# First modulation in four quarters of 256 features, each followed by its share of the latent projections

## The chip, the core and the metric

One core of a Trainium2 chip runs the kernel. The metric is the device time of one execution in microseconds; a time without a qualifier is the median of several runs. Engines are named as in the profile: PE is TensorE (matmuls; PEld its weight loads), DVE is VectorE, ACT is ScalarE, POOL is GpSimd, SP is SyncE, which here issues nearly all transfers from memory.

## The reference, cut to what matters

One layer over 256 latent and 256 context rows of 1024 features. A conditioning vector gives a shift and a scale for each feature; these modulate the normalised rows; one wide projection of the modulated rows follows, of which the 384 query columns (latent rows only) and the 320 key/value columns (all rows) are the first to be computed here. Retention, attention, a merge and 32 experts, each token using four of them, come after.

```python
m = silu(c) @ ada_w + ada_b              # 6144 columns; the first 2048 are shift and scale of this stage
h = rms_norm(x, norm1_g) * (1 + scale) + shift        # the same for ctx with its own vector
z = h @ w_in                                          # columns 6144:6528 queries, 6528:6848 key/value
```

## The kernel before

Everything is float32. A product of the big projections is made of three fast-format products: the operand is split into a high half (rounded, on ScalarE) and a low half (the rest, on VectorE), and `mm3` issues high x high, high x low and low x high. Weights come in tiles of 128 partitions x 1024 numbers into a ring of `WR = 7` buffers. `step` collects a list of steps, some with a weight; `run_steps` walks it, starts the loads up to seven weights ahead, splits a weight shortly before its use (`split_to`; `ahead[0]` says how many beyond the next, 0 in the opening and `AHEAD = 2` later, and `ahead[1](n)` calls for splits by hand), and calls the step. The instructions of each engine run in the order in which this list issues them; SP's transfers too.

The opening is written out by hand in that list. Features are counted in eight blocks of 128 (`KD = 8`).

- `ada_half(h, ks)` computes the modulation of half of the features: for each block k one weight tile of 512 shift and 512 scale columns, and two products against `sT`, which holds the two conditioning vectors in 32 columns, into `ap0[32 * g:32 * g + 32]`, g = 2h and 2h + 1. The shift goes into one strip of 32 partitions and the scale into the next. The bias comes first as a product of `ident` and `adab` in each strip. These products aren't split: an ordinary float32 product shows as two records of the trace.
- `ada_out` copies the result out of `ap0`, `ada_mod` transposes it and forms scale and shift by feature (`mod1`), and `modulate(u, ks)` makes the high and low halves `hh`, `hl` of the modulated rows (u = 0 latent, 1 context). In the code the first of these sequences is `start1`, the second `start2`.
- `norm_rows` and `xn_transposes` normalise the rows and bring them into columns.
- `project_cq` and `project_ckv` are the query and key/value projections, in steps of two blocks k.
- `keep_clock(n)` puts n small bf16 products with unused results on TensorE (`CLK`).

The order before: half 0 of the modulation, with the rows' norm and transposes between its products; `start1`; queries k 0 to 3 and key/value k 0 to 1; half 1 of the modulation, eight tiles with four dummies after each; key/value k 2 to 3 with `start2` inside; queries k 4 to 7; the queries' norm; key/value k 4 to 7; the transposes of the normed queries (`cq_rows`); the gate columns (`C_GM`) in four steps.

Later in the kernel the spaces `first` (two tiles, heads of the attention output) and `accp` (the gates) are in use; in the opening they are free. The expert weights are loaded on SP by lines 1107 and 1112 into rings of 2 MB tiles that open as the spaces of the mixer stage close.

Of the kernel before, what the change touches and what calls it, by code (L numbers as in the profile page):

```python
# [10 lines left out]
F32 = mybir.dt.float32  # L11
# [48 lines left out]
def hybrid_block(ctx: ExitStack, tc: tile.TileContext, A, out, dbg=None):  # L60
# [152 lines left out]
    def run_steps():  # L213
# [9 lines left out]
        def split_next():  # L223
            w, nk, n, raw = loaded[len(ready)]
# [13 lines left out]
        for spec, fn in steps:  # L238
            while len(loaded) < min(at[0] + WR, len(loads) - 1):
# [14 lines left out]
    def load(src, r0, nk, pieces, raw=False):  # L254

        n = sum(p[1] for p in pieces)
        w = wtile4()
        v = w[:, :nk * n].rearrange("p (k n) -> p k n", k=nk)
        o = 0
        if len(pieces) > 1 and len({p[1] for p in pieces}) == 1 and nk == 1:  # L260
            (c0, cn), (c1, _) = pieces
            a = src[r0:r0 + 128]
            a = bass.AP(tensor=a.tensor, offset=a[:, c0:c0 + cn].offset, ap=[list(a.ap[0]), [c1 - c0, 2], [1, cn]])
            nc.sync.dma_start(w[:, :n].rearrange("p (c n) -> p c n", c=2), a)
# [5 lines left out]
        return w, nk, n, raw  # L270
# [24 lines left out]
    def ada_bias(ps, r):  # L295
        nc.tensor.matmul(ps, ident[0:12, r:r + 1].to_broadcast([12, 32]), adab, start=True, stop=False)

    def ada_half(h, ks):
        for k in ks:
            def f(w, k=k):  # L300
                if h == 0 and k == 0:
                    bank("ap0")
                ap0 = B["ap0"]
# [8 lines left out]
    def ada_out(h):  # L312
        s = slice(64 * h, 64 * h + 64)
# [4 lines left out]
    def ada_mod(h):  # L318
        s = slice(64 * h, 64 * h + 64)
        ps = pt_((128, 4, 2, 32))  # L320
        for c in range(4):
            nc.tensor.transpose(ps[:, c].rearrange("p a b -> p (a b)"), ada0[s, 128 * c:128 * c + 128], ident[s, s])
        ks = slice(4 * h, 4 * h + 4)
# [1390 lines left out]
```

## Time and profile before

| what | value |
|---|---|
| median of 3 runs (lowest, highest) | 1489.52 us (1488.69, 1493.41) |
| the profiled execution: time, span | 1487.58 us, 1485.8 us |
| mean granted clock of TensorE | 0.988 |
| busy: PE, PEld, DVE, ACT, POOL | 93%, 52%, 44%, 23%, 6% |
| memory read | 490.03 MB, 331 GB/s over the span |
| L308, products of the first modulation | 64 records, 20.2 us busy |

The busy share of PE counts matmuls that are pipelined into one another, so it doesn't tell how close the engine is to its peak. A row of a timeline gives a start and a duration in us; because matmuls overlap at their ends, the price of one is read from the distance between starts. The granted clock of the first few microseconds isn't on record: 1.00 is shown there, and the distances tell more.

### The profile page before, as it was taken

What the parts mean: (1) busy time and instruction counts of PE and PEld (TensorE: products, weight loads), DVE (VectorE), ACT (ScalarE), POOL (GpSimd) and SP (SyncE); (2) the same over time, 40 slices, a digit from 0 to 9 for tenths busy, and PEclk for the clock granted to TensorE, in tenths of its full rate; (3) what the DMA queues carried; (4) which work ended last, traced back from release to release, by engine and by line L of the source; (5) the groups of instructions that cost most, each with busy time, mean ns of one, the idle gap of its engine ahead of it and who ended that gap; (6) DMA issues with size and microseconds to landing.
All of it is one profiled execution on the core that took longest, in us unless ns stands there. A gap on an engine that the chain in (4) does not pass through costs nothing.

```text
span 1485.8 us, 18943 instructions
## 1 busy us (share of the span) xinstructions
PE 1388.0 (93%) x7859; PEld 775.8 (52%) x7859; DVE 651.5 (44%) x1111; ACT 344.4 (23%) x604; POOL 87.9 (6%) x95
## 2 busy tenths in 40 slices
PE   8998999999999989999999999989899889989986
PEld 4677888888888874333333333333333333333323
DVE  4488876757676572323322323222322232223224
ACT  4364543534443331110100101100110011001001
POOL 2201050101101030000000000000000000000000
PEclk9999999999999899999999999999999999999998
DMA  8634473554548778999999999999999999999994
GB/s 286 204 108 141 142 265 101 164 177 130 176 161 322 266 286 337 427 426 427 428 425 428 427 426 427 427 428 426 427 428 426 428 427 427 427 428 427 427 422 172
DMA packets 75077, 492.38 MB, mean 331 GB/s; under 512 B 6579, under 2 KB 16892, under 8 KB 50152
## 3 DMA queue, kind: packets, MB, share of 16 engines
q1 hardware_dynamic: 74008, 489.22, 81.8%
q0 software_dynamic: 576, 1.23, 0.3%
q8 instruction: 63, 1.03, 0.3%
q10 hardware_dynamic: 400, 0.66, 0.1%
q14 instruction: 30, 0.25, 0.0%
HBM read 490.03 MB, written 1.05 MB: 331 GB/s over the span
## 4 chain that ended last, share of the span: by engine, by line
PE 51%; DMA 40%; DVE 6%; issue 1%; ACT 1%; POOL 0%; SPq 0%; DVEq 0%; ACTq 0%
DMA w<-in_exp_w_gu_dram 26%; DMA w<-in_exp_w_down_dram 13%; PE ps L1479 11%; PE ps L286 9%; PE ps L287 9%; PE ps L285 9%; PE ps L1510 5%; PE ps L145 2%; PE ps L1340 1%; PE ps L308 1%; PE ps L1459 1%; PE ps L457 1%; DVE up L1487 1%; DVE up L1485 1%; DVE ws L277 0%
## 5 line engine op out<-in xcount | busy, mean ns | idle before, releaser
L1479 PE MATMUL ps<-w,xg 128*64 128x512 f32 x2048 | 459.8, 596 | 36.2 <-DMA w<-in_exp_w_gu_dram 33.9
L1479 PEld LDWEIGHTS ps<-w,xg 128*64 128x64 f32 x2048 | 140.5, 137 | 333.8 <-issue 253.7
L1510 PE MATMUL ps<-w,ga 128*64 128x512 f32 x992 | 218.1, 592 | 0.0
L277 DVE TENSOR_TENSOR ws<-w,ws 128x1024 fp32r<-128x1024 f32 (+2 forms) x114 | 139.2, 1230 | 66.4 <-ACT ws L276 65.3
L1466 DVE SCALAR_TENSOR_TENSOR x<-ps,gate,x 128x512 f32<-128x512 f32 x124 | 84.5, 744 | 187.2 <-PE ps L1459 187.2
L1510 PEld LDWEIGHTS ps<-w,ga 128*64 128x64 f32 x992 | 71.2, 137 | 141.9 <-issue 141.9
L1519 DVE TENSOR_TENSOR ps<-ps,gate 128x512 f32<-128x512 f32 (+1 forms) x33 | 22.6, 683 | 270.1 <-PE ps L1510 261.2
L276 ACT ACTIVATE ws<-w 128x1024 fp32r<-128x1024 f32 (+2 forms) x114 | 116.9, 1028 | 101.0 <-PE ps L287 79.5
L1484 ACT ACTIVATE ps<-ga 128x512 f32<-128x512 f32 x32 | 19.3, 602 | 471.5 <-DVE ga L1483 471.5
L286 PE MATMUL ps<-ws,hh 128*128 128x512 f32 (+3 forms) x304 | 109.5, 360 | 3.5 <-DVE ws L277 3.5
L285 PE MATMUL ps<-ws,hh 128*128 128x512 f32 (+3 forms) x304 | 110.1, 362 | 2.4 <-DVE ptl L282 2.4
L287 PE MATMUL ps<-ws,hl 128*128 128x512 f32 (+3 forms) x304 | 109.1, 359 | 0.4 <-DVE hl L383 0.4
L1483 DVE TENSOR_SCALAR ga<-ps 128x512 f32<-128x512 f32 x32 | 22.1, 692 | 161.4 <-PE ps L1479 161.4
L281 ACT ACTIVATE up<-ps 128x512 fp32r<-128x512 f32 (+1 forms) x33 | 19.3, 584 | 260.2 <-DVE ps L1519 260.1
L286 PEld LDWEIGHTS ps<-ws,hh 128*128 128x128 f32 x304 | 57.3, 188 | 13.2 <-DVE ws L277 4.9
L1340 PE MATMUL ps<-bgu,ident 128*64 128x512 f32 x256 | 63.2, 615 | 0.0
L285 PEld LDWEIGHTS ps<-ws,hh 128*128 128x128 f32 x304 | 57.1, 188 | 11.4 <-DVE ptl L282 2.7
L287 PEld LDWEIGHTS ps<-ws,hl 128*128 128x128 f32 x304 | 57.1, 188 | 9.1 <-DVE hl L383 0.7
L145 PE MATMUL ps<-ident,up 128*128 128x128 f32 x128 | 24.1, 312 | 24.0 <-DVE up L1487 24.0
L340 DVE SCALAR_TENSOR_TENSOR ada<-w,sc,ada 128x1024 f32<-128x1024 f32 x32 | 40.6, 1278 | 0.0
L1426 PE MATMUL ps<-oh,acc_m 128*128 128x128 bf16 x512 | 40.6, 224 | 0.0
L285 PE MATMUL ps<-ath,hth 128*128 128x256 f32 x128 | 35.7, 279 | 1.2 <-ACT ath L281 1.2
(383 smaller groups left out, 1820.5 us busy)
## 6 DMA issues: line engine op xcount, KB each, us to landing
w<-in_exp_w_gu_dram SPq DMA_DIRECT2D x124, 2048.0 KB, 39.1
w<-in_exp_w_down_dram SPq DMA_DIRECT2D x62, 2048.0 KB, 39.1
w<-in_ada_w_dram SPq DMA_DIRECT2D x48, 512.0 KB, 4.5
w<-in_w_in_dram SPq DMA_DIRECT2D x48, 512.0 KB, 4.5
w<-in_w_in_dram SPq DMA_DIRECT2D x32, 256.0 KB, 4.3
w<-in_w_branch_ret_dram SPq DMA_DIRECT2D x16, 512.0 KB, 5.9
w<-in_exp_w_gu_dram SPq DMA_DIRECT2D x8, 1024.0 KB, 27.1
w<-in_w_branch_mla_dram SPq DMA_DIRECT2D x8, 512.0 KB, 5.2
```

The lines of the kernel that those rows point to most:

```text
L145: nc.tensor.transpose(dst, src, ident[:n, :n])
L276: nc.scalar.activation(hi[:, :n], src, AF.Copy)
L277: nc.vector.tensor_tensor(lo[:, :n], src, hi[:, :n].bitcast(F32), op=OP.subtract)
L285: nc.tensor.matmul(ps, a[0], b[0], start=start, stop=False, skip_group_check=True)
L286: nc.tensor.matmul(ps, a[0], b[1], start=False, stop=False, skip_group_check=True)
L287: nc.tensor.matmul(ps, a[1], b[0], start=False, stop=stop, skip_group_check=True)
L340: nc.vector.scalar_tensor_tensor(a, w, sc[:, k:k + 1], a, op0=OP.mult, op1=OP.add)
L1340: nc.tensor.matmul(ps[64 * h:64 * h + 64], pick_row(c // 512).to_broadcast([128, CAP]), bgu, start=True, stop=False, skip_group_check=True)
L1426: nc.tensor.matmul(ps[:, i, :w], pairs(part[:, t], 4)[:, k // 2, k % 2], rhs, start=(t + p + i == 0), stop=(t + p == 3), skip_group_check= ...
L1466: nc.vector.scalar_tensor_tensor(a, pss[h], g[:, t:t + 1], a, op0=OP.mult, op1=OP.add)
L1479: nc.tensor.matmul(ps[64 * h:64 * h + 64], xg[k // 4][:, k % 4, sl], w[:, c:c + 512], start=False, stop=(k == KD - 1), skip_group_check=True)
L1510: nc.tensor.matmul(py[64 * h:64 * h + 64], hT[f], w[:, 1024 * r + 512 * h:1024 * r + 512 * h + 512], start=(f == 0), stop=(f == KD - 1))
```

## The change

The modulation is computed in four quarters of 256 features (`ada_quarter`) instead of two halves. A weight tile now holds two blocks k of 256 shift and 256 scale columns. Shift and scale of quarter q lie side by side in one strip, `ap0[32 * q:32 * q + 32]`, and the two products of a tile, for its two blocks k, go there one after the other. The eight bias products of 256 columns all come at the start (`ada_begin`). The first six weight tiles are placed in `first` and `accp` and don't count against the seven of the ring, so the loads run further ahead; each such tile is loaded by two transfers of 256 KB. The rows are loaded ahead of all weights.

After each quarter the two blocks k that it completes are modulated (`begin(q)`), projected for the queries, and later, between the products of the next quarter, for the key/values. The dummies of the second half and of `start1` are gone. `xn_transposes` works by pairs of blocks; `cq_rows` moves behind the first gate step. The arithmetic is the same.

```diff
-            while len(loaded) < min(at[0] + WR, len(loads) - 1):
+            while len(loaded) < len(loads) - 1 and sum(not w[4] for w in loaded[at[0]:]) < WR:
...
-        w = wtile4()
+        w = where() if where else wtile4()
...
-    def ada_half(h, ks):
-        for k in ks:
-            def f(w, k=k):
...
-                for c in range(2):
-                    g = 2 * h + c
-                    if k == 0:
-                        ada_bias(ap0[32 * g:32 * g + 32], 2 * c + h)
-                    nc.tensor.matmul(ap0[32 * g:32 * g + 32], sT[:, k], w[:, 512 * c:512 * c + 512],
-                                     start=False, stop=(k == KD - 1))
-            step(f, (A["ada_w"][0], 128 * k, 1, [(512 * h, 512), (1024 + 512 * h, 512)], True))
...
+    def ada_begin():
+        bank("ap0")
+        for q in range(4):
+            for c in range(2):
+                r = 2 * c + q // 2
+                nc.tensor.matmul(B["ap0"][32 * q:32 * q + 32, 256 * c:256 * c + 256],
+                                 ident[0:12, r:r + 1].to_broadcast([12, 32]), adab[:, 256 * (q % 2):256 * (q % 2) + 256],
+                                 start=(c == 0), stop=False, skip_group_check=True)
...
+    def early_tile(n):
+
+        if n % 2 == 0:
+            early[n // 2] = (*first, accp)[n // 2].tile([128, 2, 1024], F32, name=("w", "w", "acc_m")[n // 2])
+        return early[n // 2][:, n % 2]
+
+    def ada_quarter(q, k2s):
+
+        for k2 in k2s:
+            def f(w, k2=k2):
+                for k in range(2):
+                    nc.tensor.matmul(B["ap0"][32 * q:32 * q + 32], sT[:, 2 * k2 + k], w[:, 512 * k:512 * k + 512],
+                                     start=False, stop=(2 * k2 + k == KD - 1), skip_group_check=True)
+            step(f, (A["ada_w"][0], 256 * k2, 2, [(256 * q, 256), (1024 + 256 * q, 256)], True,
+                     (lambda n=4 * q + k2: early_tile(n)) if 4 * q + k2 < 6 else None))
...
+    def begin(q):
+
+        ks = range(2 * q, 2 * q + 2)
+        ada_mod(q)
+        if q:
+            ahead[1](0)
+        modulate(0, ks)
+        ahead[1](0 if q == 0 else 1)
+        modulate(1, ks)
...
+    step(ada_begin)
     keep_clock(CLK[0])
+    step(lambda: got.__setitem__("r1", norm_factors()))
     step(gain_cols)
+    step(stash("cq"), cq_weights(0))
+    step(lambda: norm_rows(got["r1"]))
+    for k2 in range(3):
+        ada_quarter(0, range(k2, k2 + 1))
+        keep_clock(CLK[1])
+    step(lambda: xn_transposes(0))
+    ada_quarter(0, range(3, 4))
+    step(lambda: ada_out(0))
+    step(lambda: xn_transposes(1))
+    step(lambda: begin(0))
+    step(lambda: bank(*PCQ))
+    for q in range(4):
+        if q:
+            step(stash("cq"), cq_weights(q))
+        step(lambda q=q: block(cq_jobs, q, range(2), *got["cq"]))
+        if q == 3:
+            break
+        ada_quarter(q + 1, range(0, 2))
+        if q == 0:
+            step(lambda: (xn_transposes(2), xn_transposes(3), bank(*PKV)))
+        step(stash("kv"), kv_weights(q))
+        step(lambda q=q: block(kv_jobs, q, range(1), *got["kv"]))
+        ada_quarter(q + 1, range(2, 4))
+        step(lambda q=q: ada_out(q + 1))
+        step(lambda q=q: block(kv_jobs[:2], q, range(1, 2), *got["kv"]))
+        step(lambda q=q: begin(q + 1))
+        step(lambda q=q: block(kv_jobs[2:], q, range(1, 2), *got["kv"]))
     step(lambda: ahead.__setitem__(0, AHEAD))
...
     step(cq_norm)
-    project_ckv(range(2, 4))
+    step(lambda hi, lo: block(kv_jobs, 3, range(2), hi, lo), kv_weights(3))
+    project_lat(C_GM, ("gm0", "gm1"), range(0, 1))
     step(cq_rows)
-    project_lat(C_GM, ("gm0", "gm1"), range(0, 1))
     step(ckv_norm)
```

## Rows read from the trace of the kernel before

**Rows 1.** Page, part 2: GB/s moved in 40 equal slices
```profile
GB/s 286 204 108 141 142 265 101 164 177 130 176 161 322 266 286 337 427 426 427 428 425 428 427 426 427 427 428 426 427 428 426 428 427 427 427 428 427 427 422 172
```

**Rows 2.** Page, part 4: chain that ended last, shares of the span
```profile
PE 51%; DMA 40%; DVE 6%; issue 1%; ACT 1%; POOL 0%; SPq 0%; DVEq 0%; ACTq 0%
```

**Rows 3.** Stretches: length, busy us (instructions) per engine, PEclk, DMA share, GB/s
```profile
600.00:1000.00 400.00, 384.74 (x2158) 150.06 (x2156) 120.44 (x199) 44.08 (x97) 0.00 (x0) 1.00 1.01 427
```

**Rows 4.** Stretches of the opening, the same view
```profile
4.00:30.00 26.00, 25.66 (x178) 12.41 (x178) 8.15 (x28) 11.24 (x18) 1.86 (x4) 1.00 1.01 348
...
40.40:53.80 13.40, 13.40 (x71) 3.37 (x69) 0.95 (x2) 0.74 (x1) 0.00 (x0) 1.00 0.53 169
```

**Rows 5.** TensorE's waits, 0 to 70 us: us in total, times, longest
```profile
PE ps L286 <- DVE ws L277: 2.0, 3, 0.9
...
PE ps L308 <- DMA w<-in_ada_w_dram: 0.2, 1, 0.2
```

**Rows 6.** Timeline, SP: start, us, instruction, count
```profile
461.02 5.86 SPq L1107 DMA_DIRECT2D w<-in_exp_w_gu_dram  x3
```

**Rows 7.** SP's waits, 440 to 600 us
```profile
SPq L1107 <- PE ps L287: 14.8, 4, 4.5
```

**Rows 8.** Timeline, TensorE, second half; of xN records two make a product
```profile
40.48 1.04 PE L296 MATMUL ps<-adab,ident 12*32 12x512 f32 x2
41.45 1.04 PE L308 MATMUL ps<-w,sT 128*32 128x512 f32 x2
...
44.38 0.40 PE L457 MATMUL ps<-ones 128*128 128x128 bf16 x4
44.70 1.05 PE L308 MATMUL ps<-w,sT 128*32 128x512 f32 x4
45.69 0.40 PE L457 MATMUL ps<-ones 128*128 128x128 bf16 x4
```

**Rows 9.** Timeline, TensorE, first half: two pairs, then transposes
```profile
21.20 1.91 PE L308 MATMUL ps<-w,sT 128*32 128x512 f32 x8
23.05 1.97 PE L145 MATMUL ps<-ident,x 128*128 128x128 f32 x16
```

**Rows 10.** Timeline, TensorE: two full-width products and the next line
```profile
487.98 1.88 PE L1190 MATMUL ps<-ada,one 128*128 128x512 f32 x4
489.78 1.08 PE L1195 MATMUL ps<-ada,one 128*64 128x512 f32 x4
```

**Rows 11.** Timeline, TensorE, start: product, bias product, sixty dummies
```profile
5.98 1.89 PE L308 MATMUL ps<-w,sT 128*32 128x512 f32 x2 [0.18 <-DMA w<-in_ada_w_dram]
7.80 1.91 PE L296 MATMUL ps<-adab,ident 12*32 12x512 f32 x2
...
11.49 4.06 PE L457 MATMUL ps<-ones 128*128 128x128 bf16 x60
```

**Rows 12.** Timeline, first joint: copy-out, transposes, low half, dense product
```profile
27.44 0.41 DVE L315 COPY ada<-ps 64x256 f32<-64x256 f32 x1
...
27.99 0.71 PE L322 MATMUL ps<-ident,ada 64*128 64x64 f32 x4
...
29.08 0.96 DVE L277 TENSOR_TENSOR ws<-w,ws 128x768 fp32r<-128x768 f32 x1
...
30.96 0.44 PE L287 MATMUL ps<-ws,hl 128*128 128x384 f32 x1 [0.42 <-DVE hl L383]
```

**Rows 13.** Timeline, TensorE: last two latent products
```profile
69.99 0.31 PE L286 MATMUL ps<-ws,hh 128*128 128x320 f32 x1
...
70.13 0.31 PE L287 MATMUL ps<-ws,hl 128*128 128x320 f32 x1
```

**Rows 14.** Timeline, TensorE: the fourth gate block
```profile
82.19 0.50 PE L286 MATMUL ps<-ws,hh 128*128 128x512 f32 x1 [1.50 <-DVE ws L277]
```

**Rows 15.** Timeline, TensorE: first product after an idle stretch
```profile
142.93 0.58 PE L286 MATMUL ps<-ptl,mvh 128*128 128x256 f32 x1 [2.93 <-DVE ptl L282]
```

**Rows 16.** Stretches again, here for the granted clock (PEclk)
```profile
142.00:146.00 4.00, 3.07 (x15) 3.08 (x16) 3.94 (x6) 0.32 (x1) 0.00 (x0) 0.57 0.79 265
```

More of the change, by code (lines that the diff above doesn't have):

```diff
@@ L223, in split_next @@
         def split_next():
[L224 removed]
+            w, nk, n, raw, _ = loaded[len(ready)]
             if raw:
@@ L252, in run_steps, with load @@
         steps.clear()
-    def load(src, r0, nk, pieces, raw=False):
+    def load(src, r0, nk, pieces, raw=False, where=None):
         n = sum(p[1] for p in pieces)
-        w = wtile4()
+        w = where() if where else wtile4()
         v = w[:, :nk * n].rearrange("p (k n) -> p k n", k=nk)
         o = 0
-        if len(pieces) > 1 and len({p[1] for p in pieces}) == 1 and nk == 1:
+        if len(pieces) > 1:
             (c0, cn), (c1, _) = pieces
-            a = src[r0:r0 + 128]
-            a = bass.AP(tensor=a.tensor, offset=a[:, c0:c0 + cn].offset, ap=[list(a.ap[0]), [c1 - c0, 2], [1, cn]])
-            nc.sync.dma_start(w[:, :n].rearrange("p (c n) -> p c n", c=2), a)
+            for k in range(nk):
+                a = src[r0 + 128 * k:r0 + 128 * k + 128]
+                a = bass.AP(tensor=a.tensor, offset=a[:, c0:c0 + cn].offset, ap=[list(a.ap[0]), [c1 - c0, 2], [1, cn]])
+                nc.sync.dma_start(v[:, k].rearrange("p (c n) -> p c n", c=2), a)
         else:
@@ L269, in load @@
                 o += cn
-        return w, nk, n, raw
+        return w, nk, n, raw, where
     def split(src, n):
@@ L357, in norm_rows, with xn_transposes @@
                 nc.vector.tensor_scalar(xt, xt, r1[:, t:t + 1], None, op0=OP.mult)
-    def xn_transposes(u):
-        for k2 in range(KD // 2):
+    def xn_transposes(k2):
+        for u in range(2):
             ps = pt_((128, 2, 256))
@@ L385, in modulate, with project, block @@
                 nc.gpsimd.dma_start(dbg["hT"][:, k, s], hf)
-    def project(pieces, jobs, kks, mid=None, at=None):
+    def project(pieces, jobs, kks):
         for k2 in kks:
-            def f(hi, lo, k2=k2):
-                for k in range(2):
-                    kk = 2 * k2 + k
-                    for n, (name, cut, t, a, b, first) in enumerate(jobs):
-                        if mid and at == (k, n):
-                            mid()
-                        s = slice(128 * t, 128 * t + 128)
-                        mm3(cut(B[name]), (hh[:, kk, s], hl[:, kk, s]), (hi[:, k, a:b], lo[:, k, a:b]),
-                            start=(kk == 0 and first), stop=(kk == KD - 1))
-            step(f, (A["w_in"][0], 256 * k2, 2, pieces))
+            step(lambda hi, lo, k2=k2: block(jobs, k2, range(2), hi, lo), (A["w_in"][0], 256 * k2, 2, pieces))
+    def block(jobs, k2, ks, hi, lo):
+        for k in ks:
+            kk = 2 * k2 + k
+            for name, cut, t, a, b, first in jobs:
+                s = slice(128 * t, 128 * t + 128)
+                mm3(cut(B[name]), (hh[:, kk, s], hl[:, kk, s]), (hi[:, k, a:b], lo[:, k, a:b]),
+                    start=(kk == 0 and first), stop=(kk == KD - 1))
     def whole(p):
```

83 lines of the change are left out of this document (24 added, 59 removed).

## The prediction

> **What bounds the kernel now.** I read the slices of the span first, then the opening stretch by stretch, then who made TensorE wait there, then single instructions. In the slices [rows 1] the transfers run near 427 GB/s only from about the sixteenth slice on; before that they move 100 to 340 GB/s. The chain of work that ended last says the same: about half TensorE, four tenths transfers of expert weights [rows 2]. So there are two regimes, an opening and a mixer bound by the order written for TensorE, and then an expert stage bound by bytes (427 GB/s, transfers busy all the time [rows 3]).
>
> The change lies wholly in the first 75 us. There TensorE is busy for 25.66 of the 26 us from 4 to 30 and for all of the 13.4 us from 40.4 to 53.8, while the transfers make 348 and 169 GB/s [rows 4]. Before 70 us it waited 0.2 us for a weight of the first modulation, and 2.0 us for split weights [rows 5]. The opening is thus bound by how long TensorE's list is, not by the weights' arrival: whatever the change gains by earlier transfers has next to nothing to remove. What counts is whether the new list is longer.
>
> Does a longer opening reach the end? The expert transfers are issued on SP when space falls free: the first three at 461 us, in 5.9 us [rows 6], and between 440 and 600 us SP waited 14.8 us for TensorE's last mixer products before issuing four of them [rows 7]. So the start of the byte-bound regime moves with TensorE, and I carry a delay of the opening to the end one to one.
>
> **The change, part by part.** All prices are of the profiled execution: span 1485.8, time 1487.58 us.
>
> (a) The modulation's products. A product here has 32 columns of stationary data and 512 columns to stream. Before, line 308 issues two for each weight tile, into different strips of 32 partitions. At full clock such a pair takes 0.98 us when something else stands ahead of it (44.70 to 45.69), and two pairs in a row take 1.85 (21.20 to 23.05), so each further one 0.86 [rows 8, 9]. A lone one takes 0.97 (40.48 to 41.45, a bias product of 512 columns; the two of line 308 beside it take as long) [rows 8]. So the second of a pair is free: the strips run side by side. After the change the two products of a tile go into the same strip, 32q, one after the other. Two full-width products in a row, which can't share the array, take 1.80 us between 487.98 and the next line's start at 489.78 [rows 10], that is 0.95 and 0.86. So there are still 32 products, but none is free.
> Before: two lone ones on the low clock, 1.82 each (5.98 to 7.80 [rows 11]), seven pairs of the first half, 3 x 0.98 + 2 x 1.85, then two lone and seven pairs of the second, 2 x 0.97 + 7 x 0.98; in all 19.1 us. After: 32 x 0.86, and ten fresh starts (four in the first quarter, two in each other) at 0.12 (0.98 less 0.86) are 28.7 us. Difference **+9.6**. Bounds: 32 x 0.86 bare is +8.4, 32 x 0.97 is +11.9.
>
> (b) The bias products: four of 512 columns become eight of 256, all at the start on the low clock. Before: 2 x 1.82 + 2 x 0.97 = 5.6 us. After: eight at half of 1.82 are 7.3 us in single file. Neighbours at a change of q lie in different strips; if these overlap as the pairs of line 308 do, five slots, 4.6 us. The first weight tile then sets the limit: 2.1 MB of rows, 0.39 of the query weight and 0.52 of its own stand ahead of the first product, at 348 GB/s [rows 4] 8.7 us after transfers begin near 3.5, so 12.5 to 13.5. I take the overlap, capped by that: **-0.5**, with +1.8 as the other end. The rows alone don't settle it: a bias product and a product of line 308 in different strips did not overlap (5.98, 7.80 [rows 11]), but they differ in rows (12 and 128), as bias neighbours do not.
> The Trainium skill bears on this place: TensorEngine Tiling (Array Packing), section "Key Properties", says that tiles work independently and that a change of tiling mode drains the engine. By it the bias products, all of one mode, would overlap (the 4.6), and by the row of unlike neighbours taken alone they would not (the 7.3); the two sums differ by 2.3 us.
>
> (c) Dummies. The second half's eight groups of four vanish, 0.32 each (44.38 to 44.70 [rows 8]), and one group of six more appears in the first quarter, some 0.4 (six of the sixty that take 4.06 at the start [rows 11]). **-2.1**. The 30 dummies inside the old first joint filled a wait and are counted there.
>
> (d) The joints, where products of the modulation become scale and shift and these become activations. Before, the first joint runs from the copy-out at 27.44 to the third dense product at 30.96, 3.5 us [rows 12], with later waits of some 1.4 for split weights (of the 2.0 in [rows 5]); the second, its transposes and a wait, I estimate at 1.6. In all 6.5. After there are four. The pieces [rows 12]: copy-out 0.41 and its other half after it, transposes (0.71 with their wait for that half, some 0.5 without), then 2.26 us from their end (28.70) to the product at 30.96, 0.96 of it a weight's low half queued first on VectorE. In quarter 0 that split is done earlier and the copy-out lies beside eight transposes (half of 1.97 [rows 9]): 0.5 + 1.3. In quarters 1 to 3 six dense products of 0.15 (69.99 to 70.13 [rows 13]) hide the copy-out, six more (0.88) part of the 2.26; the weight split stands ahead of the activations on ScalarE and VectorE again, so 0.5 + 1.4 each. Queued behind these waits on TensorE are the query products of the quarter, and behind them the next quarter's narrow products, which would have been ready. One wait is new: the first key/value weight is split only at its own step, behind the last copies of the transposed rows, and TensorE stands right behind it: copy 0.6, high half 0.8, low half 0.8 (estimates from 0.96 for a wider tile), 2.2 us. Sum 1.8 + 5.7 + 2.2 = 9.7, so **+3.2**; bounds +0.5 (the splits fall beside other work) and +6 (each joint as dear as the old first one).
>
> (e) The tail. The transposes of the query rows now stand behind the first gate block instead of ahead of it, so the squares of the key/value latents on ScalarE start later, and the fourth gate block, which already waits 1.5 us at 82.19 [rows 14], some later still: **+1**, between 0 and 1.5.
>
> At nothing: the six tiles in space used later (that space is next written after 75 us), the doubled number of weight transfers (two of 256 KB each; SP is not what TensorE waits for, and only quarter 0 could feel a slower rate, 2.3 us of work for each 0.52 MB, 228 GB/s), and the smaller copies and transposes of x, moved but the same in sum. Were the pieces to come at half of 348 GB/s, quarter 0 would lose some 3 us.
>
> Sum: 9.6 - 0.5 - 2.1 + 3.2 + 1.0 = **+11.2 us**: 1498.8 for an execution like the profiled one. The median of the runs, 1489.52, is 1.9 above that; against it, **1500.7**, and that is the predicted time. Ends by the bounds: +6.3 (8.4 - 0.5 - 2.1 + 0.5 + 0) to +19.1 (11.9 + 1.8 - 2.1 + 6 + 1.5), so 1495.8 to 1508.6.
>
> **The rivals.** One: a strip takes its second product at the price of a pair's share, 0.43. Then (a) is 32 x 0.43 + 1.2 - 19.1 = -4.1, and the sum -2.5: 1487, not slower. It decides below 0.51 us a product, where the sum is nought. Against it: the lone products at 0.97 and line 1190 [rows 8, 10]; for it: no row has two narrow products in one strip. 4%.
> Two: the clock falls. The narrow products now run 3.5 us at a stretch, six times, with the dummies that stood between them gone. At 142.93 us TensorE came back from 2.93 us without work [rows 15], and the granted clock of 142 to 146 us is 0.57 in the mean [rows 16]: nearly all of it at 1.2 instead of 2.4 GHz, about 1.4 of the 2.9 us from 142.93 lost. A fall on a run of narrow products would cost up to 3.5. Two or three falls: about 1506. For it: from 5.98 to 11.49 nothing but narrow products ran and the clock stayed at the lower level (1.82 us a product for 0.97), until the 60 dummies [rows 11]. Against it: the 3.9 us of lone products from 40.48 kept full speed [rows 8]. 15%. The Trainium skill, TensorE: Matmul & The Clock Gate, section "What's actually happening", says that the clock follows how busy the engine has been; by it alone a list without idle time never falls, and this rival would be nought. The start of this trace differs: a busy engine stayed slow.
> Three: the delay is swallowed before the experts, because their first transfers wait for something not in TensorE's order. 1490, no change. Against it the waits of SP [rows 7]. 7%.
> Four: the change doesn't do what it says: the weights still come late, since SP waits for a split before the fourteenth load and all later ones queue behind it. TensorE would wait in quarters 1 to 3; with some 3 us, 1503.5. By the order of issue each tile is there before its turn. 5%.
>
> **How the numbers follow.** My forecast (sum +6 to +19) has 69%, the rivals 4, 15, 7 and 5. The range takes in the sum's bounds and most of the clock's case and leaves out the two that are not slower: 1495 to 1509. About 0.3% (4.5 us) is what a measurement of this kernel can tell from no change: faster by more: 3% (the low side of rival one); within that: 10% (rivals one and three); slower: 87%.
>
> **What would show it.** In the changed kernel's timeline, narrow products start 0.43 apart for each pass, never two together; the last latent product ends near 80 us, for 70.1 before [rows 13]; waits of TensorE for split weights and activations before 80 us come to some 7 us for 2.7; the expert transfers start about 11 us later. The prediction is wrong if two products of one strip overlap, if the bias products and joints sum to far less, or if the first expert transfer is issued as early as before.

## The result and the profile after

| | before | after |
|---|---|---|
| median, us | 1491.47 | 1511.0 |
| lowest to highest, us | 1488.69 to 1493.81 | 1505.63 to 1511.41 |
| the profiled execution: time, span, us | 1487.58, 1485.8 | 1511.41, 1509.6 |
| mean granted clock | 0.988 | 0.980 |

The ratio after to before is 1.0126, with a 95% interval from 1.0106 to 1.0146. The change makes the kernel slower, as forecast, but by some 19 us and not by 11: the measured 1511.0 lies above the upper end of the range, 1509. Executions of one kernel differ by some 5 us, before the change as after it. One execution of a kernel further down (`rows_tail_fill`) took 3618.91 us, for a reason that isn't known; the kernel's median is 1500.36 with it and 1500.21 without it.

Four instants split each trace into stages: the start of the last key/value product, the start of the first product that uses the queries' rows (`cqh`), and SP's issue of the first three expert loads; the span is the fourth.

| us | opening, to the last key/value product | tail, from there to the first use of `cqh` | mixer, from there to the expert loads | the rest |
|---|---|---|---|---|
| before | 70.1 | 14.7 | 376.2 | 1024.8 |
| after | 80.1 | 24.9 | 379.3 | 1025.3 |
| difference | +9.95 | +10.2 | +3.2 | +0.5 |

The opening came close to its forecast (10.2, which is the sum without the tail's 1.0). TensorE in the changed kernel (start, us, instruction, count, the wait ahead of it in brackets); in the first four lines a product is two records:

```profile
3.88 1.95 PE L301 MATMUL ps<-adab,ident 12*32 12x256 f32 x16
12.71 1.88 PE L318 MATMUL ps<-w,sT 128*32 128x512 f32 x4 [1.58 <-DMA w<-in_ada_w_dram]
27.05 3.62 PE L318 MATMUL ps<-acc_m,sT 128*32 128x512 f32 x8
...
36.84 4.95 PE L318 MATMUL ps<-w,sT 128*32 128x512 f32 x8
...
80.08 0.31 PE L288 MATMUL ps<-ws,hl 128*128 128x320 f32 x1
```

The next line starts at 30.61, 3.56 us behind the four narrow products at 27.05. That is 0.89 each: nothing is shared, where [rows 9] has four in 1.85. The run at 36.84 takes 4.95 because the clock was low there. The last latent product starts at 80.08, for 70.13 in [rows 13]. TensorE's waits from 0 to 82 us (us in total, times, longest), which answer [rows 5] (a first wait of 3.7 us, for the inputs, is the same in both kernels and left out):

```profile
PE ps L318 <- DMA w<-in_ada_w_dram: 1.6, 1, 1.6
PE ps L286 <- ACT ws L277: 1.3, 1, 1.3
PE ps L288 <- DVE hl L396: 1.3, 3, 0.4
PE ps L286 <- ACT hh L394: 1.0, 1, 1.0
PE ps L287 <- DVE ws L278: 0.4, 1, 0.4
```

They are 5.6 us, some 1.6 of it for the first weight tile; the joints and the first key/value weight wait 4.0 us in all.

The surplus begins right behind. The same view, the tail:

```profile
80.23 0.39 PE L286 MATMUL ps<-ws,hh 128*128 128x512 f32 x1
84.58 0.79 PE L287 MATMUL ps<-ws,hh 128*128 128x512 f32 x1 [3.97 <-DVE ws L278]
85.18 0.63 PE L288 MATMUL ps<-ws,hl 128*128 128x512 f32 x1
85.60 0.63 PE L286 MATMUL ps<-ws,hh 128*128 128x512 f32 x1
...
97.46 1.09 PE L145 MATMUL ps<-ident,pth 128*128 128x128 f32 x8 [0.94 <-ACT pth L593]
...
100.76 0.62 PE L287 MATMUL ps<-ws,hh 128*128 128x512 f32 x1 [1.50 <-DVE ws L278]
```

The first gate product has its high half of the weight, and the second waits 3.97 us for the low half. The products behind it stand 0.43 us apart; at the higher clock it is 0.23. In the kernel before, the tail's only wait is the 1.50 us of [rows 14]. The stretches of the changed kernel in which the clock was low (length, busy us and instructions of PE, PEld, DVE, ACT, POOL, then granted clock, DMA share, GB/s), with that wait as the second line:

```profile
36.20:39.60 3.40, 3.40 (x7) 1.03 (x7) 0.00 (x0) 0.00 (x0) 0.00 (x0) 0.51 0.38 131
80.30:84.60 4.30, 0.33 (x3) 0.02 (x1) 4.23 (x20) 1.06 (x1) 0.70 (x2) 0.92 0.02 4
83.90:90.80 6.90, 6.21 (x18) 5.05 (x19) 3.38 (x4) 0.00 (x0) 0.00 (x0) 0.51 0.56 190
101.00:104.40 3.40, 3.40 (x9) 2.62 (x9) 2.31 (x5) 1.81 (x4) 0.00 (x0) 0.50 0.75 239
162.40:169.30 6.90, 6.24 (x26) 6.05 (x27) 4.65 (x9) 1.31 (x3) 0.00 (x0) 0.51 0.60 209
268.30:271.70 3.40, 3.40 (x18) 3.40 (x17) 0.83 (x1) 0.00 (x0) 0.00 (x0) 0.50 0.40 114
```

Before 300 us the kernel before has one such stretch, around [rows 16]. Here there are five, 24 us long together. The one at 83.9 begins in the wait of 3.97 us, and the one at 101.0 right behind three waits of 0.94, 0.22 and 1.50 us. In the kernel before, the 1.50 us alone was followed by none. At half clock, about half of TensorE's busy time in such a stretch is lost.

The tail's +10.2 can be added up from these rows. Its waits are 6.6 us instead of 1.5, which is +5.1. Half of TensorE's busy time in the two low stretches, 6.2 and 3.4 us, is 4.8 more.

Why is the low half late? The first fence shows the changed kernel: the start of the queries' norm on VectorE, the gate weight's low half there, the clearing on GpSimd, and the first of the key/value products that cover the norm. The second shows the same four in the kernel before (two low halves in one row), and the gate product that needs the low half:

```profile
78.08 2.37 DVE L154 TENSOR_SCALAR rs_v<-sq 128x2 f32<-128x2 f32 x1 [0.66 <-ACT t2k L560]
...
83.31 1.22 DVE L278 TENSOR_TENSOR ws<-w,ws 128x1024 fp32r<-128x1024 f32 x1
...
76.91 3.52 POOL L340 MEMSET ada<- 128x4096 f32 x1
...
76.71 0.31 PE L286 MATMUL ps<-ws,hh 128*128 128x320 f32 x1
```
```profile
64.09 1.31 DVE L154 TENSOR_SCALAR rs_v<-sq 128x2 f32<-128x2 f32 x1 [0.25 <-ACT t2k L540]
...
68.26 2.35 DVE L277 TENSOR_TENSOR ws<-w,ws 128x1024 fp32r<-128x1024 f32 x2
...
61.85 3.52 POOL L329 MEMSET ada<- 128x4096 f32 x1
...
63.24 0.31 PE L285 MATMUL ps<-ws,hh 128*128 128x320 f32 x1
...
71.17 0.39 PE L286 MATMUL ps<-ws,hh 128*128 128x512 f32 x1
```

The first instruction of the queries' norm handles two numbers in each partition and takes 2.37 us. It ends at 80.45, 0.02 behind the clearing of `ada` on GpSimd; in the kernel before it ends at 65.40, 0.03 behind it. The norm's chain stands on VectorE ahead of the gate weight's low half. Before, two key/value steps (7.0 us of products) covered that chain; now one does (3.5 us). Counted from the first key/value product of that cover, TensorE came to the low half after 7.93 us before and comes to it after 3.90 now (84.58 less the wait); the half us beside the missing step is the transposes of the query rows, which now stand behind. VectorE began the low half, 1.2 us of work, after 5.02 us before and after 6.60 now.

The expert loads follow, 23.3 us later than in [rows 6]:

```profile
484.29 5.86 SPq L1127 DMA_DIRECT2D w<-in_exp_w_gu_dram  x3
```

### The profile page after: what moved, and what is told of

The parts are those of the page before. It is cut to its first block, busy times and chain, and to the rows that moved or that the text cites. A ratio compares the mean times of both kernels' runs of the same rounds, so it can differ in the third digit from the quotient of the medians.

```text
span 1509.6 us, 18877 instructions
## 1 busy us (share of the span) xinstructions
PE 1404.4 (93%) x7819; PEld 785.8 (52%) x7819; DVE 653.7 (43%) x1117; ACT 345.7 (23%) x606; POOL 88.8 (6%) x95
## 3 DMA queue, kind: packets, MB, share of 16 engines
q0 software_dynamic: 576, 1.23, 0.3%
q8 instruction: 63, 1.03, 0.3%
## 4 chain that ended last, share of the span: by engine, by line
PE 51%; DMA 40%; DVE 7%; ACT 1%; issue 1%; POOL 0%; SPq 0%; DVEq 0%; ACTq 0%; POOLq 0%
DMA w<-in_exp_w_gu_dram 26%; DMA w<-in_exp_w_down_dram 13%; PE ps L1499 11%; PE ps L288 9%; PE ps L287 9%; PE ps L286 9%; PE ps L1530 5%; PE ps L145 2%; PE ps L318 2%; PE ps L1360 1%; DMA w<-in_ada_w_dram 1%; PE ps L1479 1%; DVE ws L278 1%; DVE up L1507 1%; DVE up L1505 1%
## 5 line engine op out<-in xcount | busy, mean ns | idle before, releaser
L1486 DVE SCALAR_TENSOR_TENSOR x<-ps,gate,x 128x512 f32<-128x512 f32 x124 | 84.5, 744 | 185.5 <-PE ps L1479 185.5
L278 DVE TENSOR_TENSOR ws<-w,ws 128x1024 fp32r<-128x1024 f32 (+1 forms) x114 | 139.2, 1230 | 54.2 <-ACT ws L277 53.3
L277 ACT ACTIVATE ws<-w 128x1024 fp32r<-128x1024 f32 (+1 forms) x114 | 116.7, 1028 | 84.0 <-PE ps L288 81.4
L286 PE MATMUL ps<-ws,hh 128*128 128x512 f32 (+3 forms) x304 | 112.5, 370 | 4.9 <-DVE ptl L283 2.4
L287 PE MATMUL ps<-ws,hh 128*128 128x512 f32 (+3 forms) x304 | 111.4, 366 | 5.9 <-DVE ws L278 5.9
L288 PEld LDWEIGHTS ps<-ws,hl 128*128 128x128 f32 x304 | 58.1, 191 | 10.8 <-DVE hl L396 2.2
```

The source lines that it names most:

```text
L277: nc.scalar.activation(hi[:, :n], src, AF.Copy)
L278: nc.vector.tensor_tensor(lo[:, :n], src, hi[:, :n].bitcast(F32), op=OP.subtract)
L286: nc.tensor.matmul(ps, a[0], b[0], start=start, stop=False, skip_group_check=True)
L287: nc.tensor.matmul(ps, a[0], b[1], start=False, stop=False, skip_group_check=True)
L288: nc.tensor.matmul(ps, a[1], b[0], start=False, stop=stop, skip_group_check=True)
L1486: nc.vector.scalar_tensor_tensor(a, pss[h], g[:, t:t + 1], a, op0=OP.mult, op1=OP.add)
```

## The experiments

All times are medians; the stages are those of the table above, from one profiled execution each. Every kernel computes the same result.

| kernel | us | ratio to before, 95% interval | opening | tail | mixer |
|---|---|---|---|---|---|
| before | | 1 | 70.1 | 14.7 | 376.2 |
| after | 1511.0 | 1.0126 [1.0106, 1.0146] | 80.1 | 24.9 | 379.3 |
| tail_split | 1504.66 | 1.0096 [1.0079, 1.0113] | 80.4 | 20.8 | 376.9 |
| memset_early | 1505.14 | 1.0097 [1.0079, 1.0115] | 78.3 | 22.3 | 379.7 |
| fill_wait | 1505.63 | 1.0104 [1.0087, 1.0121] | 78.9 | 23.0 | 377.2 |
| two_strips | 1507.0 | 1.0097 [1.0075, 1.012] | 76.2 | 23.0 | 381.5 |
| rows_back | 1502.95 | 1.0092 [1.0073, 1.0111] | 78.5 | 19.5 | 378.0 |
| rows_tail | 1501.67 | 1.0078 [1.006, 1.0096] | 80.4 | 18.1 | 379.4 |
| ring_only | 1506.93 | 1.0111 [1.0091, 1.0132] | 78.7 | 25.2 | 381.6 |
| four_strips_tail | 1483.46 | 0.9953 [0.9935, 0.9971] | 63.6 | 16.5 | 376.9 |
| rows_tail_fill | 1500.36 | 1.0066 [1.0048, 1.0084] | 80.7 | 16.6 | 376.3 |
| four_strips | 1495.17 | 1.0028 [1.0015, 1.004] | 64.5 | 24.9 | 379.6 |
| before_memset | 1490.94 | 1.0009 [0.9997, 1.0022] | 71.4 | 14.7 | 377.7 |
| four_strips_fill | 1480.55 | 0.9941 [0.9923, 0.996] | 61.8 | 16.6 | 375.3 |

The rest, from the first expert loads to the end, is 1023.1 to 1025.3 us in all of them. The median of the kernel before was 1490.51 beside the first four kernels, 1489.18 beside the next four and 1489.11 beside the last four, so the ratios are what is compared across these groups. The intervals of tail_split, memset_early, fill_wait, two_strips, rows_back and ring_only all overlap that of the changed kernel: what a single repair gains is near the noise, and it is the traces that show causes there. Clear of it are rows_tail, rows_tail_fill and the kernels with four strips.

The openings of 80.1 to 80.7 us have the low clock at 36 us; those of 78.3 to 78.9 don't, with the same list for TensorE and the same waits ahead of that place. That difference belongs to none of the edits.

### tail_split: the gate weight split ahead of the norm

```diff
+    step(lambda: ahead[1](1))
     step(cq_norm)
```

> The changed kernel with one call more: the first gate weight is split just ahead of the queries' norm instead of behind it. Theory (the surplus over the forecast comes from the tail: the gate weight's low half is late because the norm's VectorE chain stands ahead of it and only 3.5 us of key/value products cover it, and the 4.0 us of wait then drop TensorE's clock): the wait of 3.97 us at 80.6 falls under 1 us, the run at half clock from 83.9 to 90.8 goes with it, and the kernel gains 7 to 10 us: some 1501 to 1504, about 1.007 of the kernel before. Rival A (the clock falls because of the narrow products and the missing dummies, not because of the wait): the wait goes, the low clock stays, gain about 3 to 4 us, some 1507. Rival B (something that the norm needs is late anyway, the norm moves back by what the split moves forward): no gain, some 1510.

```profile
80.51 0.39 PE L286 MATMUL ps<-ws,hh 128*128 128x512 f32 x1
80.74 0.39 PE L287 MATMUL ps<-ws,hh 128*128 128x512 f32 x1
...
92.97 1.09 PE L145 MATMUL ps<-ident,pth 128*128 128x128 f32 x8 [2.49 <-ACT pth L593]
...
96.29 0.79 PE L287 MATMUL ps<-ws,hh 128*128 128x512 f32 x1 [1.21 <-DVE ws L278]
```

The wait is gone, and so is the low clock behind it: gate products 0.23 apart. The ratio falls by 0.0030 (some 4.5 us), less than the theory had. What it missed: 10 us further on TensorE waits for the key/value norm (2.49, for 0.94 in the changed kernel), then for the fourth gate weight, and the clock is low there from 94.2 to 101.1. Rival A is out for the first stretch.

### memset_early: GpSimd's clearing moved to the first step

```diff
-        ada_start()          # in cq_norm
+    step(ada_start)          # ahead of load_rows
```

> The changed kernel with the clearing of the later modulation's buffer on GpSimd (3.52 us, at 76.9 in the changed kernel, at 61.9 before) moved to the first step of the list. Theory (a small VectorE instruction of the queries' norm, 2.37 us for 128x2 elements, was held for as long as GpSimd's clearing ran, since both ended within 0.03 us of each other): the instruction takes about 0.2 us, the gate weight's low half comes 2.2 us earlier, the wait of 3.97 us becomes about 1.8, and the kernel gains at least 2 us, up to 7 if the shorter wait no longer drops the clock: 1504 to 1508. Rival (the instruction is slow for a reason of its own, such as its operands in PSUM): it still takes over 2 us and nothing is gained, some 1510.

```profile
76.33 0.17 DVE L154 TENSOR_SCALAR rs_v<-sq 128x2 f32<-128x2 f32 x1 [0.66 <-ACT t2k L560]
```
```profile
80.63 0.50 PE L287 MATMUL ps<-ws,hh 128*128 128x512 f32 x1 [1.75 <-DVE ws L278]
```

0.17 instead of 2.37 us, and the wait of 3.97 becomes 1.75, as the theory said: the clearing held the small instruction. Even 1.75 us was followed by a low clock (81.1 to 84.5), half as long as in the changed kernel. At the next waits, of 1.23, 0.22 and 1.50 us, it is low again, from 94.7 to 101.6.

### fill_wait: TensorE kept busy through the wait

```diff
-    project_lat(C_GM, ("gm0", "gm1"), range(0, 1))
+    step(lambda: bank("gm0", "gm1"))
+
+    def fill_wait():
+        for _ in range(64):
+            nc.tensor.matmul(B["gm0"][:, :128], ones, ones, start=True, stop=True)
+    step(fill_wait)
+    project([(C_GM, 512)], [(n, whole, t, 0, 512, True) for t, n in enumerate(("gm0", "gm1"))], range(0, 1))
```

> The changed kernel with 64 small products without a use ahead of the first gate product, so that TensorE is busy through most of the wait of 3.97 us; the wait itself stays. Theory (the wait drops the clock, the low clock costs about as much again): the gate products behind it run at full speed, 0.23 us apart instead of 0.43, and the kernel gains 3 to 5 us, some 1506. Rival (the clock would fall there without a wait too, because of what ran before): the gate products stay at 0.43, no gain, some 1510.

```profile
79.01 3.75 PE L643 MATMUL ps<-ones 128*128 128x128 bf16 x64
82.57 0.47 PE L286 MATMUL ps<-ws,hh 128*128 128x512 f32 x1
83.34 0.50 PE L287 MATMUL ps<-ws,hh 128*128 128x512 f32 x1 [0.30 <-DVE ws L278]
```
```profile
79.00:92.00 13.00, 12.70 (x107) 10.82 (x106) 9.71 (x33) 3.56 (x11) 0.75 (x2) 1.00 0.31 104
95.60:102.40 6.80, 5.44 (x14) 4.38 (x15) 4.89 (x8) 3.34 (x8) 0.00 (x0) 0.50 0.48 157
```

The second fence shows two stretches. Up to 92 us the clock is 1.00, though the gate weight comes as late as ever; it falls at 95.6, at the next waits. The same list with the wait left empty fell in the changed kernel and in ring_only, both times for 6.9 us. So the wait set the clock, not what ran ahead of it. That is the trace of one execution; over the six, the mean granted clock is 0.983 to 0.987, for 0.980 to 0.985 in the changed kernel. The gain of 0.0022 in the ratio is within the noise.

### two_strips: the two products of a tile side by side

```diff
-    matmul(ap0[32 * q:32 * q + 32], sT[:, 2 * k2 + k], w[:, 512 * k:512 * k + 512], ...)
+    r = 32 * (2 * (q % 2) + k)
+    matmul(ap0[r:r + 32], sT[:, 2 * k2 + k], w[:, 512 * k:512 * k + 512], ...)
...
-    nc.tensor.transpose(ps[:, c // 2, c % 2], ada0[s, 128 * c:128 * c + 128], ident[s, s])
+    nc.tensor.matmul(ps[:, c // 2, c % 2], ada0[s, 128 * c:128 * c + 128], sel[s], start=True, stop=True)
```

The bias is added on VectorE; 110 dummies stand at the start instead of 60 and the bias products.

> The changed kernel with the two products of each tile sent to two different strips of 32 partitions of the array, so that they can run side by side; the two partial sums are added by the product that brings scale and shift into columns, and the bias is added there on VectorE instead of by products. Same order of steps, same weights. Theory (term a: two products of one strip run one after the other, 0.43 a pass, and that alone is +9.6 us of the opening): a tile costs about 1.0 instead of 1.90 us, 16 tiles some 13 to 14 us less, the last latent product ends near 66 to 69 us instead of 80.1, and unless the tail takes it back the kernel comes to 1496 to 1499. Rival (the opening is bound by the arrival of weights or by the joints, and the strips don't matter): TensorE waits for weights instead, the last latent product stays near 78 to 80 us, some 1510.

```profile
63.14 1.91 PE L325 MATMUL ps<-w,sT 128*32 128x512 f32 x8
64.98 0.41 PE L286 MATMUL ps<-ws,hh 128*128 128x320 f32 x1
...
66.06 1.07 PE L340 MATMUL ps<-sel,ada 64*128 64x32 f32 x8
67.07 0.41 PE L286 MATMUL ps<-ws,hh 128*128 128x320 f32 x1
```
```profile
25.10:28.60 3.50, 3.50 (x12) 2.66 (x12) 1.11 (x3) 0.65 (x2) 1.03 (x2) 0.51 1.08 347
35.40:38.80 3.40, 3.40 (x11) 1.38 (x12) 0.00 (x0) 0.00 (x0) 0.00 (x0) 0.50 0.49 150
55.90:59.30 3.40, 3.40 (x10) 3.01 (x10) 1.82 (x4) 0.91 (x2) 2.03 (x2) 0.50 0.36 104
69.50:72.90 3.40, 3.40 (x11) 3.40 (x12) 1.75 (x4) 1.45 (x5) 3.40 (x3) 0.50 1.01 298
```

Four products in 1.84 us instead of 3.56: the price per tile is as the theory has it. Yet the opening gained 3.9 us, not 11 to 14. A joint costs 1.0 us where its transposes took 0.36, in quarter 0 the first two tiles still take 1.6 and 2.2 us, as their weights come, and the clock fell four times in the opening, 13.7 us of which half is lost. The mechanism was right and the size of the gain was not.

### rows_back: the query rows' transposes ahead of the first gate block again

```diff
+    step(cq_rows)
     project_lat(C_GM, ("gm0", "gm1"), range(0, 1))
-    step(cq_rows)
```

> The changed kernel with one move undone: the transposes of the normed query rows stand ahead of the first gate block again. Theory (their place matters: behind the gate block they hold back the squares of the key/value latents on ScalarE, so the fourth gate block waits and the clock falls once more; ahead of it they wait themselves for the norm, which has only 3.5 us of cover): TensorE waits some 3 us for the norm ahead of the transposes and less than 1 us for the gate weight; the last gate block comes without the wait of 1.2 to 1.5 us and without low clock. About 2 to 5 us less than the changed kernel, 1505 to 1508. Rival (the move is worth nothing, the wait only changes its place, and the clock falls behind it all the same): some 1510.

```profile
81.41 1.20 PE L145 MATMUL ps<-ident,t2k 128*128 128x128 f32 x6 [2.60 <-DVE t2k L565]
82.27 0.77 PE L286 MATMUL ps<-ws,hh 128*128 128x512 f32 x1
82.98 0.80 PE L287 MATMUL ps<-ws,hh 128*128 128x512 f32 x1
```

One line moved back takes the tail from 24.9 to 19.5 us. TensorE now waits 2.6 us for the norm, and the gate weight is there when it comes to it. The wait for the norm has its low clock too (the products at 82.27 and 82.98 are 0.71 apart): the granted clock is 0.50 from 82.2 to 85.6. The fourth gate weight still waits 1.50 us, against the theory, but the clock did not fall behind it. The gain, 0.0034 of the ratio or some 5 us, is about the largest that the theory had.

### rows_tail: the three repairs together

> The changed kernel with three repairs of the stretch behind the last latent product together: the transposes of the query rows ahead of the first gate block again, the first gate weight split ahead of the queries' norm, and the clearing of the later buffer on GpSimd moved to the first step. The opening itself stays. Theory (the surplus over the forecast of 11 us lies in that stretch and in the low clock behind its waits; the opening costs +10 by itself): the delay against the kernel before is about 10 us at the last latent product and still 10 to 12 us when the mixer begins; 1500.5 to 1503. Rival A (the clock falls in this stretch because of the opening, whatever the waits): waits shorter, low clock stays, some 1505 like either repair alone. Rival B (the clock falls far later in the mixer are a matter of their own and cost 3 us more in any case): 1503 to 1505 with delays that still grow after 140 us.

The opening is still 10.3 us longer than before, the tail 18.1 us, the ratio 1.0078: in the theory's range, and almost the forecast's (1500.7 to 1489.52 is 1.0075). TensorE waits 0.80 us ahead of the query rows and not at all for the first gate weight; behind 1.7 us of waits at 92 to 94 us the clock falls from 94.5 to 97.9. Rival B holds for part of it: in the profiled execution (1504.74, the longest of them) the clock fell again at 155.9 and 261.7.

### ring_only: no tile in space used later

```diff
-    (lambda n=4 * q + k2: early_tile(n)) if 4 * q + k2 < 6 else None
+    None
```

> The changed kernel with all weight tiles of the modulation in the ring of seven, none in space used later. Theory (the opening is bound by TensorE's list, the early loads have nothing to remove): as the changed kernel within 2 us, 1508 to 1512, the last latent product near 80 us. Rival (the six tiles in other space are what keeps TensorE fed in the first two quarters, as the list needs 2 weights for each 4 products now): waits for weights of several us in quarters 0 and 1, 1514 or more.

1506.93, ratio 1.0111, which can't be told from the change's 1.0126. TensorE waited 1.4 us for weights of the modulation, once. The early tiles are worth nothing here, as their term in the forecast had it.

### four_strips_tail and four_strips: all four strips, with and without the repairs

```diff
-    r = 32 * (2 * (q % 2) + k)
+    r = 32 * ((2 * k2 + k) % 4)
```

The edit is shown against two_strips, cut to the line that picks the strip. The first kernel also has the repairs of rows_tail and splits the first key/value weight ahead of the context's activations.

> The changed kernel with the products of a pair of tiles spread over all four strips of the array (partial sums added by the product that brings scale and shift into columns, bias added on VectorE), with the three repairs of the stretch behind the last latent product, and with the first key/value weight split ahead of the context's activations. Theory (what the change loses is one strip for all products; the rest is order): a run of four products takes about 1.0 us instead of 3.55, the opening loses 4 x 2.6 us and more, the last latent product comes near 64 us (70.1 before, 80.1 in the changed kernel) as long as the clock holds, and the kernel ends at 1484 to 1490, level with or ahead of the kernel before. Rival A (short narrow products let the clock fall at each joint, as the run with two strips showed four times): some 5 us dearer, 1491 to 1496. Rival B (weights become the bound): TensorE waits for weights in quarters 1 to 3, 1491 to 1496 too, but with those waits in the trace.

> The changed kernel with the products of a pair of tiles spread over all four strips of the array, as in the run with four strips before, but with nothing else altered behind the last latent product and in the first key/value split. Theory (strips and the stretch behind are two separate terms, 16 to 17 us and 8 to 9 us): the last latent product near 64 to 66 us, the wait for the gate weight of 2 to 4 us and the low clock behind it as in the changed kernel; 1490 to 1494, no better than the kernel before. Rival (the repairs were worth little once the opening is short): 1484 to 1486, like the run with both.

The run with the repairs:

```profile
40.07 1.06 PE L325 MATMUL ps<-w,sT 128*32 128x512 f32 x8
41.06 0.41 PE L286 MATMUL ps<-ws,hh 128*128 128x320 f32 x1
...
63.55 0.30 PE L288 MATMUL ps<-ws,hl 128*128 128x320 f32 x1
```

Four products in 0.99 us. With the repairs the kernel is faster than the one before, 0.9953 [0.9935, 0.9971]. Without them it is a little slower, 1.0028, and 1495.17 is just above the theory's 1490 to 1494. Its tail is 24.9 us like that of the changed kernel, with a wait of 3.96 us for the gate weight, so the two causes stand side by side. In the profiled executions the strips are worth 15.6 us of the opening, 1.7 of it the low clock at 36 us, and the repairs 8.3 of the tail.

### rows_tail_fill and four_strips_fill: products without a use in the waits that are left

```diff
+            for _ in range(12 if t == 0 else 0):           # in cq_rows
+                nc.tensor.matmul(ps[:, 0], ones, ones, start=True, stop=True)
...
+            for _ in range(24 if u else 5):                # in ckv_rows
+                nc.tensor.matmul(ps[:, 0, 0:128], ones, ones, start=True, stop=True)
...
+    keep_clock(18)           # four_strips_fill only, behind begin(0)
```

> The run with the three repairs of the stretch behind the last latent product, and 65 small products without a use in the waits that are left there (12 ahead of the transposes of the query rows, 5 and 24 ahead of those of the key/value rows). The waits themselves stay. Theory (what the stretch still loses, 1.5 us between 92 and 98 us, is the low clock that follows two waits; keep TensorE busy there and it is gone): no low clock between 80 and 110 us, the delay against the kernel before stays at 11 to 12.5 us up to 140 us, the kernel gains 1 to 2 us, 1499.5 to 1501. Rival A (the later falls at 156 and 262 us are chance and decide the rest): no low clock between 80 and 110, but no gain that can be told from 1501.7. Rival B (the products only add to TensorE's list): 1502 to 1504.

> The run with four strips and the three repairs, with small products without a use in its waits: 18 behind the first joint, where the clock fell at 25.4 us, and 12, 5 and 24 in the stretch behind the last latent product. Theory (the falls at 25.4 and 107.3 us follow waits): both low stretches vanish, 2 to 3 us less, 1480 to 1482. Rival (the falls come from the short narrow products and selector products, not from the wait): the fall in the opening stays, 1483 to 1485.

A stretch of rows_tail_fill, then one of four_strips_fill:

```profile
80.00:110.00 30.00, 29.30 (x207) 25.65 (x206) 25.01 (x67) 16.11 (x32) 0.00 (x0) 1.00 0.53 157
```
```profile
4.00:70.00 66.00, 63.69 (x470) 48.34 (x470) 33.95 (x101) 30.92 (x59) 18.77 (x17) 1.00 0.85 272
```

The granted clock is 1.00 in both stretches, as expected, and the tail is 16.6 us. The first kernel is 1.3 us shorter than rows_tail, where the theory put it, though the two intervals overlap. The second, at 0.9941 of the kernel before, is the fastest by its median, though its interval overlaps that of four_strips_tail; its clock doesn't fall once before the expert loads.

### before_memset: the clearing moved in the kernel before

> The kernel before with the clearing of the later buffer on GpSimd (3.52 us at 61.85) moved to the second step of its list, nothing else. Theory (a small VectorE instruction beside the clearing is held until it ends; in the kernel before that was hidden behind 6.9 us of key/value products): the first instruction of the queries' norm on VectorE takes 0.2 us instead of 1.31, TensorE's order does not move by more than 0.5 us, and the time stays within 0.15% of 1489. Rival (the kernel before pays for it too): 1 to 2 us faster.

```profile
65.38 0.17 DVE L154 TENSOR_SCALAR rs_v<-sq 128x2 f32<-128x2 f32 x1 [0.32 <-ACT t2k L540]
```

The instruction takes 0.17 us instead of 1.31, the tail stays 14.7 us, the ratio 1.0009 holds 1 in its interval. The opening is 1.3 us longer, where the theory allowed 0.5: the sixty dummies near its start took 5.5 us for 4.06, for a reason that isn't shown. The kernel before had the same fault and did not pay for it in the tail.

## Why the prediction was right or wrong

**What bounds the kernel, and the carry to the end: right.** Weights played no part (ring_only), and the expert stage is the same length within 0.5 us. The carry of one to one missed the mixer's own 3.2 us; rival three is out. So is rival four: behind the first tile TensorE waited for no weight of the modulation.

**(a) The products of one strip: right.** Worked out from the distances between starts, the narrow products took 19.15 us before and 29.96 after, +10.8 for +9.6 forecast; 1.3 of it is the low clock at 36.84. Rival one is out: 0.89 us each, and two and four strips bring four products from 3.56 us to 1.84 and 0.99.

**(b), (c), (d): right in sum, wrong apart.** The same reckoning gives, before and after: bias products 5.69 and 1.88, dummies 9.20 and 6.12, joint transposes 1.03 and 1.50, dense products 24.39 and 26.90 (more fresh starts, some low clock), waits 2.76 and 5.56, transposes of rows 4.40 and 4.64. With the 10.8 that is the 9.95. These three terms were to give +0.6 and gave -0.9. The bias ran four strips abreast, quicker than the 4.6 us taken, but the cap by the first weight held: its product starts at 12.71, inside 12.5 to 13.5. The joints were overestimated: the waits for split weights and activations, forecast at some 7 us, were 4.0 (5.6 with the first weight tile), and the first key/value weight cost 1.8 instead of 2.2. That the opening meets its 10.2 is in part luck: 1.7 us of the 9.95 is the low clock at 36 us, which no term of the sum had and which four of the kernels with the same list don't show.

**(e) The tail: this step failed.** It was sized at +1, between 0 and 1.5, and measured +10.2. The step followed one instruction group, the transposes of the query rows, to one later wait. What it followed came near its size: 0.94 and 0.22 us of new waits ahead of the fourth gate block, whose own wait stayed 1.50. Of the other 9 us, 3.97 are the wait for the gate weight and some 4.8 the low clock. It left out three things that the rows and the diff had in them. First, the diff takes one of the two key/value steps from behind the queries' norm; so the norm and the low half of the gate weight, queued behind it on VectorE, lost half of their cover. That is the order of a queue, not a price, and it was not looked at (with the weight split ahead of the norm, tail_split, the wait is gone). Second, an instruction of 1.31 us for two numbers stood in the trace of before, hidden by that cover; where the cover goes, it comes out, and at 2.37 (memset_early, before_memset): 2.2 of the 3.97 us. Third, [rows 15, 16] showed that a wait costs again in the clock behind it. The forecast used this for a rival only and not for each new wait; behind 3.97 us it was a low clock of 6.9 us, and with TensorE kept busy it was none (fill_wait). Undoing the move (rows_back) and repairing all (rows_tail_fill) bring the tail to 19.5 and 16.6. That rows_tail ends on the forecast's ratio doesn't bear the forecast out: its tail is still +3.4 and its mixer, in the profiled execution, +3.2.

**Rival two: its price was right, its place was not.** It had up to 3.5 us a fall, and the falls here cost 1.7 or some 3.1; but the fall was expected on runs of narrow products. One did come in the opening, at 36.2 us, in dense products behind 1.8 us of waits; in four of the changed openings (memset_early, fill_wait, rows_back, ring_only) none came behind the same waits. The falls in the tail stood at its waits. The Trainium skill, TensorE: Matmul & The Clock Gate, "What's actually happening", has the clock follow how busy the engine has been; fill_wait and four_strips_fill agree, with 1.00 where the waits were filled.

**What stays open.** The falls at 162 and 268 us stand far behind the change. Counted as in the tail they cost some 4.8 us, for some 1.4 of the one fall of the kernel before, and that is about the mixer's 3.2. They are there in some kernels and not in others, with the same list of work from 105 us on; executions of the changed kernel itself lie 5.8 us apart, those of the kernel before 5.1. What decides them was not found, nor why the same wait is followed by a low clock in one execution and not in another. Together with the tail's surplus of 9.2 they make the difference between 11 and the 23.8 us of the profiled execution.

## What to carry to other kernels

Where a diff thins out the work behind which a chain runs on another engine, list what is queued on that engine behind the chain and compare the new cover with its whole length, including the instructions that were slow and hidden before. Put a price on the clock behind each new wait of TensorE, not on the wait alone, even though some waits here had no low clock behind them. Where narrow products must be made, give neighbours different strips: four of 512 columns took 3.56 us in one strip, 1.84 in two and 0.99 in four.

## What the runs showed of the hardware

The small VectorE instruction (`TENSOR_SCALAR`, 128x2) is shown as running, not as waiting, until GpSimd's clearing ends; instructions with two operands ran at their usual length beside it (0.42 us for 128x256, at 77.00 us as at 76.19 ahead of it). The Trainium skill, SBUF — State Buffer, "SBUF: two separate sides", describes a port pair of the two engines that one of them holds for a whole instruction; this trace agrees (2.37 us beside the clearing, 0.17 without), and its exception for operations with two inputs beside a clearing, which reads nothing, agrees too.

The eight bias products of 256 columns took 1.9 us. At the lower clock, which the kernel before shows at that place (1.82 us for 512 columns, [rows 11]), single file would have been 7.3, and 1.9 is the time of two in a row: the four strips ran abreast although the order gives each strip its two products one behind the other. And 1.75 us without work was followed by a low clock (memset_early), while 1.50 was not in the profiled executions of rows_back and of the kernel before.
